# A two-layer hybrid backbone: S5 output operators on VectorE, and the second layer's operators made in the first layer's output projection

## The chip, the cores and the metric

The kernel runs on one core of one Trainium2 chip. The metric is device time in microseconds of one launch; each number of a run is the time of that one core. TensorE is called PE, VectorE DVE, ScalarE ACT, GpSimd POOL, and SyncE, which here only issues transfers, SP.

## The reference

Two layers over 256 context and 512 latent tokens of width 1024. Each layer normalises and modulates, projects into three groups of heads (SSD, GLA, S5), runs a scan in both directions in each, and projects the concatenation back with a gate and a residual. The change concerns the S5 group: 32 groups of 16 channels, each with 64 complex states per direction.

```python
lam_bar = jnp.exp(lam * jnp.exp(log_step[d])[:, None])
b_bar = ((lam_bar - 1.0) / lam)[..., None] * bmat
...
bu = jnp.einsum("blgh,gph->blgp", u.astype(jnp.complex64), b_bar)
h = s5_scan(bu, h0, lam_bar)      # h_t = lam_bar * h_{t-1} + bu_t
return jnp.einsum("blgp,ghp->blgh", h, cmat).real, h[:, -1]
...
for l in range(DEPTH):
    u_lat = rmsnorm(h_lat, norm_w[l]) * (1.0 + scale[:, None]) + shift[:, None]
    ...
    out_lat = jnp.concatenate([ssd_l, gla_l, s5_l], axis=-1) @ w_out[l]
    h_lat = h_lat + gate[:, None] * out_lat
return rmsnorm(h_lat, final_norm_w)
```

## The kernel before, in words

Everything is kept transposed, channels on the 128 partitions and tokens along the free axis. A product in 32 bits is three matmuls, since each operand is split into a high and a low part: `wsplit` (L409 to L417) loads a weight tile `wr` of 512 KB (L412), ACT copies it into `wh` (the copies of all helpers are recorded on L121), and a subtraction makes `wl` (L416), two times in three on POOL and once on DVE. The input projection's matmuls are L492 (latent tokens, tile `pl`) and L494 (context, `pc`), those of the output projection L1062 and L1064.

The S5 scan is done in blocks of eight tokens, 96 blocks in all. For that, operators are made from the parameters:

- `s5_lambda` (L253 to L349): some hundred small DVE operations that make the table of powers of `lam_bar`, `s5p` (128x576), and `l8` for the scan; PE transposes the powers, and they go to memory (`lpD`, L340).
- `s5_in_map` (L351 to L363), eight per layer: two loads of 512 KB (B, with each row sent to many partitions, and the powers), then six DVE operations of 128x512 (L360, L361 and L363, each twice). The result is the operator from eight tokens to a state; the matmuls L608 apply it, and DVE (L612, L613) and ACT put the result into the scan's tile `xy`.
- `s5_out_map` (L365 to L404), sixteen per layer: a load of C and B (L370), POOL's negation of a piece (L375) and six POOL operations of 128x288 that multiply the table with C (L380 to L385), a store of the result (`clD`, L388), 16 small PE matmuls (L394) into two tiles of the pool `pa` for the kernel inside a block of eight tokens, two ACT copies, two small DVE operations (L400, L401) and two stores (`gD`, L403 and L404). All of a map lies in one tile of the pool `cs`, which has three buffers.
- the scan itself is `carry` (L643 to L646) on DVE; the output matmuls L687 to L689 reload `clD` and `gD`.

Where things stand in the program: layer 0's eight input maps come ahead of its input projection, in the tiles `bA` and `bB`, with two tiles of the pool `bc` for their loads. Inside layer 0's input projection (L571 to L580) layer 1's lambda and eight input maps are made, in `bA`, and spilled to memory (`pwD`, `blD`); layer 1 loads them again (L602, L617). Layer 0's sixteen output maps come behind the loads of u (L594 to L596). Layer 1's sixteen output maps come behind layer 0's S5 output (L694 to L696), with the table loaded again (L669).

The output projection (`out_part`, L1053) has two halves. The first, over GLA and S5 channels, leaves partial sums in memory (`hpD`); then 16 rows of layer 1's modulation are made (L1089 to L1095); the second half is a loop over eight output blocks m (L1098 to L1114), each with a weight load, its matmuls, the partial sum's load and the residual on DVE (L1075, L1076). Then come the rest of the modulation, the norm of layer 1 (`norm_in`, L441) and layer 1 itself.

The order on each engine is not written by hand: a scheduler places the instructions when the kernel is built, by their order in the program and by when it takes their operands and buffers to be free. Once built, each engine goes through its instructions in that order. All loads and stores stand in SP's one queue, in order too.

Of the kernel before, what the change touches and what calls it, by code (L numbers as in the profile page):

```python
# [41 lines left out]
def hybrid_backbone_kernel(  # L42
# [17 lines left out]
    dma = nc.sync.dma_start  # L60
# [128 lines left out]
    pwD = dram([128, 704], "pwD1")  # L189
    blD = dram([8, 128, 1024], "blD1")  # L190
# [46 lines left out]
    pw0, l8_0 = T("s5p", [128, 576], 1), T("l8", [128, 128], 1)  # L237
# [126 lines left out]

    def s5_out_map(l, bi, pw, buf):  # L365

        gs = 2 * bi
        w5, tmp, cb, cn = cuts(buf, 576, 288, 128, 32)
# [9 lines left out]
        cr, ci, cm = (x.rearrange("p (g h) -> p g h", g=2).unsqueeze(2).to_broadcast(shp)  # L378
                      for x in (cb[:, 0:32], cb[:, 32:64], cn))
# [96 lines left out]
    def layer(l, u):  # L476
# [94 lines left out]
        wa = wa0 if not last else big("bA")  # L571
        if not last:
            sv, wk, lt, tw, tu, pwl = cuts(wa, 480, 512, 512, 576, 576, 704)
# [20 lines left out]
        if not last:  # L594
            for bi in range(16):
                s5_out_map(0, bi, pw_(pw0), cs())  # L596
        st = T("xy", [128, 8, NT], 1).rearrange("p a t -> p (a t)").rearrange("p (i r g) -> p i r g", i=96, r=2)
        for bi in range(16):
            if bi % 2 == 0:
                blt = bls[bi // 2] if not last else wa[:, 4096 + 1024 * (bi // 2 % 2) : 5120 + 1024 * (bi // 2 % 2)]  # L600
                if last:
                    dma(blt, blD[bi // 2])  # L602
            bl = blt.rearrange("p (a g x) -> p a g x", a=2, g=4)[:, :, 2 * (bi % 2) : 2 * (bi % 2) + 2, :]
# [10 lines left out]
        l8t = l8_0  # L614
        if last:
            l8t = T("l8", [128, 128], 1)
            dma(l8t, pwD[:, 576:704])  # L617
# [642 lines left out]
```

## Time and profile before

| | us |
|---|---|
| median of 3 runs (lowest, highest) | 1706.68 (1698.17, 1707.37) |
| the profiled execution | 1712.97 |
| its span | 1711.3 |
| PE busy | 1418.1 (83%) |
| DVE busy | 1168.2 (68%) |
| POOL busy | 783.2 (46%) |
| ACT busy | 679.9 (40%) |

The mean clock that PE was granted is 0.901 of its full speed. Busy shares are averages over stages with different limits. The stages that matter here, by time in the span: layer 0's input projection with the making of S5 operators, from 45 us on; a stretch from 480 to 640 us in which layer 1's output maps are made beside projections; layer 0's output projection, whose first half ends at about 943 us and whose second half ends at 1022; the norm of layer 1; and layer 1's projections and S5 scan behind it.

### The profile page before, as it was taken

The page shows a single profiled execution, that of the slowest core. Times are in us where ns is not written, and L with a number is a line of the kernel's source. Part 1 is how long each engine was busy: PE and PEld are TensorE (multiplying, and loading weights), DVE is VectorE, ACT ScalarE, POOL GpSimd, SP SyncE. Part 2 cuts the span into 40 slices and gives each one's busy share as a digit, 9 for nine tenths or more (in the row PEclk, how much of TensorE's full clock was granted, in tenths as well). Part 3 has the DMA queues.
Part 4 walks back from the last instruction along what each step waited for, and adds up shares of the span by engine and source line. Part 5 has one row for each costly group of instructions (what it writes and reads, how often), then busy time and mean ns, then how long its engine had stood idle before and what let it go on. Part 6 is the DMA issues. An engine that isn't in the chain of part 4 may idle for free.

```text
span 1711.3 us, 23539 instructions
## 1 busy us (share of the span) xinstructions
PE 1418.1 (83%) x8536; PEld 1145.2 (67%) x8536; DVE 1168.2 (68%) x1992; ACT 679.9 (40%) x1220; POOL 783.2 (46%) x716
## 2 busy tenths in 40 slices
PE   3867766888989779977779999997889989967886
PEld 2656655777966557755668786886678777745665
DVE  7977558995477567679994127289835986688752
ACT  4312223225342336646553124343345345545442
POOL 3615647632268843445463141164123323656454
PEclk9788987898988889988889999998988999988998
DMA  8474654332543354444455745522363242344542
GB/s 308 124 185 135 178 150 135 93 118 71 176 123 86 100 165 140 142 154 139 128 187 188 282 135 178 189 85 80 111 193 107 64 139 93 119 138 145 184 131 96
DMA packets 139885, 243.55 MB, mean 142 GB/s; under 512 B 31992, under 2 KB 72568, under 8 KB 139768
## 3 DMA queue, kind: packets, MB, share of 16 engines
q1 hardware_dynamic: 139768, 242.04, 45.3%
q8 instruction: 67, 1.10, 0.3%
q14 instruction: 50, 0.41, 0.1%
HBM read 192.81 MB, written 49.18 MB: 141 GB/s over the span
## 4 chain that ended last, share of the span: by engine, by line
PE 25%; DVE 18%; DMA 13%; POOL 6%; issue 4%; ACT 4%; SPq 0%; DVEq 0%; ACTq 0%; POOLq 0%
PE pl L492 7%; PE pl L1062 6%; DMA bA<-acsD 5%; DMA bB<-acsD 3%; PE pc L494 2%; PE pc L1064 2%; DVE xy L863 1%; DMA wr<-in_wblk 1%; ACT bA L121 1%; POOL wl L416 1%; DVE bB L916 1%; DVE bA L916 1%; DVE xy L645 1%; DMA cs<-zD 1%; DVE bA L644 1%
## 5 line engine op out<-in xcount | busy, mean ns | idle before, releaser
L492 PE MATMUL pl<-hl,wh 128*128 128x512 f32 (+1 forms) x1184 | 411.5, 414 | 15.9 <-DVE ev L511 12.3
L416 POOL TENSOR_TENSOR wl<-wr,wh 128x1024 fp32r<-128x1024 f32 (+1 forms) x82 | 210.4, 2566 | 308.5 <-ACT wh L121 284.6
L492 PEld LDWEIGHTS pl<-hl,wh 128*128 128x128 f32 (+1 forms) x1184 | 226.0, 195 | 73.5 <-DVE ev L511 13.6
L492 PE MATMUL pl<-hl,wl 128*128 128x512 f32 (+1 forms) x592 | 243.5, 412 | 20.0 <-POOL wl L416 10.7
L121 ACT ACTIVATE wh<-wr 128x1024 fp32r<-128x1024 f32 (+1 forms) x122 | 127.6, 1047 | 283.7 <-PE pc L1064 69.3
L494 PE MATMUL pc<-hl,wh 128*128 128x256 f32 (+1 forms) x864 | 202.0, 304 | 11.3 <-DVE ev L511 7.2
L494 PEld LDWEIGHTS pc<-hl,wh 128*128 128x128 f32 (+1 forms) x864 | 152.5, 202 | 26.1 <-DVE ev L511 8.7
L492 PEld LDWEIGHTS pl<-hl,wl 128*128 128x128 f32 (+1 forms) x592 | 115.4, 195 | 49.1 <-POOL wl L416 12.0
L494 PE MATMUL pc<-hl,wl 128*128 128x256 f32 (+1 forms) x432 | 128.6, 298 | 0.0
L1062 PE MATMUL pl<-hl,wh 128*128 128x512 f32 x256 | 87.7, 419 | 16.9 <-ACT hl L121 4.6
L394 PE MATMUL pa<-cs 64*32 64x128 f32 x512 | 42.9, 305 | 64.0 <-POOL cs L382 27.3
L494 PEld LDWEIGHTS pc<-hl,wl 128*128 128x128 f32 (+1 forms) x432 | 87.3, 202 | 2.7 <-issue 1.7
L121 ACT ACTIVATE ev<-pl 128x512 f32<-128x512 f32 (+1 forms) x96 | 51.1, 534 | 87.7 <-PE pl L709 43.9
L709 PE MATMUL pl<-wh,hl 128*128 128x256 f32 x384 | 79.6, 307 | 2.6 <-ACT ev L121 2.6
L416 DVE TENSOR_TENSOR wl<-wr,wh 128x1024 fp32r<-128x1024 f32 x40 | 55.4, 1386 | 38.3 <-ACT wh L121 38.1
L121 ACT ACTIVATE bB<-bB 128x512 f32<-128x512 f32 (+4 forms) x40 | 45.7, 1142 | 85.1 <-DMA bB<-acsD 52.3
L394 PEld LDWEIGHTS pa<-cs 64*32 64x32 f32 x512 | 21.5, 115 | 80.6 <-POOL cs L382 28.9
L863 DVE SCALAR_TENSOR_TENSOR xy<-ev,par_sb,xy 128x512 f32<-128x512 f32 (+1 forms) x112 | 74.8, 704 | 0.6
L375 POOL TENSOR_SCALAR cs<-cs 128x32 f32<-128x32 f32 x32 | 20.1, 629 | 118.4 <-DMA cs<-in_s5cb 43.3
L709 PEld LDWEIGHTS pl<-wh,hl 128*128 128x128 f32 x384 | 66.9, 214 | 7.8 <-ACT ev L121 3.8
L1062 PEld LDWEIGHTS pl<-hl,wh 128*128 128x128 f32 x256 | 49.8, 199 | 31.1 <-ACT hl L121 6.7
L709 PE MATMUL pl<-wl,hl 128*128 128x256 f32 x192 | 58.4, 308 | 3.8 <-DVE wl L416 3.8
(483 smaller groups left out, 3604.4 us busy)
## 6 DMA issues: line engine op xcount, KB each, us to landing
wr<-in_wblk SPq DMA_DIRECT2D x80, 512.0 KB
wr<-in_wout SPq DMA_DIRECT2D x32, 512.0 KB
hl<-in_mod_w SPq DMA_DIRECT2D x20, 512.0 KB
bA<-acsD SPq DMA_DIRECT2D x10, 1024.0 KB
bB<-acsD SPq DMA_DIRECT2D x10, 1024.0 KB
clD<-cs SPq DMA_DIRECT2D x64, 128.0 KB
cs<-clD SPq DMA_DIRECT2D x32, 256.0 KB
cs<-in_mod_w SPq DMA_DIRECT2D x16, 512.0 KB
```

Source lines behind the costliest of these rows:

```text
L121: return S.activation(out, in_, f, **kw)
L375: G.tensor_scalar(cn, cb[:, 0:32], -1.0, None, MUL)
L394: PE.matmul(pk[d][32 * gg : 32 * gg + 32], b0[64 * d : 64 * d + 64, a, :], w54[64 * d : 64 * d + 64, a, gg, d : 8 + d, :].rearrange("p k h ...
L416: (eng or (V if wcount[0] % 3 == 0 else G)).tensor_tensor(wl, wr, wh.bitcast(F32), SUB)
L492: PE.matmul(p_l[:m], lhs, u[k][:, ui, LC:NT], start=st, stop=sp)
L494: PE.matmul(p_c[:m], lhs, u[k][:, ui, 0:LC], start=st, stop=sp)
L644: V.tensor_tensor(tr[:, 1, :n], li, src[:, :, ::-1], MUL)
L709: PE.matmul(p, u[k][:, ui, 128 * c : 128 * c + 128], ws[k // 4][wi][:, 256 * (k % 4) : 256 * (k % 4) + 256], start=n == 0, stop=n == 23)
L863: V.scalar_tensor_tensor(ac, raw[:, o + k : o + k + n], pcol("cw", w0 + k), ac, MUL, ADD)
L916: V.scalar_tensor_tensor(rf[:, h, :], rbw[:, h, :], rb[:, ih : ih + 1], rf[:, h, :], SUB, MIN)
L1062: PE.matmul(p_l, lhs, rhs[kk][:, ui, LC - t0 : NT - t0], start=st, stop=sp)
L1064: PE.matmul(p_c, lhs, rhs[kk][:, ui, 0:LC], start=st, stop=sp)
```

## The change

It has four parts. (1) The six operations of `s5_out_map` go from POOL to DVE; the negation falls away, because the last operation, a `scalar_tensor_tensor`, now multiplies by −1. (2) Layer 1's lambda moves behind layer 1's first modulation rows, ahead of the second half of layer 0's output projection; its tables stay in SBUF (`s5p`, `l8`), with the tile `m12` for scratch. (3) Layer 1's eight input maps are made at the head of layer 1, behind its norm, by the same function as layer 0's (`s5_in_maps`), into `bA` and `bB`. They take both tiles of the pool `bc`, so that the loads of u, which use these tiles, come after. The spilled copies `pwD` and `blD` are gone. (4) Layer 1's sixteen output maps are made two by two in the loop over m of the second half of layer 0's output projection.

```diff
-    pwD = dram([128, 704], "pwD1")
-    blD = dram([8, 128, 1024], "blD1")
...
-    pw0, l8_0 = T("s5p", [128, 576], 1), T("l8", [128, 128], 1)
+    s5p = [(T("s5p", [128, 576], 1), T("l8", [128, 128], 1))]
...
+    def s5_in_maps(l):
+        t = [bct(), bct()]
+        wa, wb = big("bA"), big("bB")
+        out = [wb[:, 1024 * i : 1024 * i + 1024] for i in range(6)] + [wa[:, 1024 * i : 1024 * i + 1024] for i in range(2)]
+        for bi in range(8):
+            s5_in_map(l, bi, t[bi % 2][:, 0:1024], t[bi % 2][:, 1024:1536], wa[:, 2048:2560], out[bi])
+        return out
...
-        G.tensor_scalar(cn, cb[:, 0:32], -1.0, None, MUL)
...
-        G.tensor_tensor(w54[:, 0], pr, cr, MUL)
-        G.tensor_tensor(t54, pi, ci, MUL)
-        G.tensor_tensor(w54[:, 0], w54[:, 0], t54, SUB)
-        G.tensor_tensor(w54[:, 1], pi, cm, MUL)
-        G.tensor_tensor(t54, pr, ci, MUL)
-        G.tensor_tensor(w54[:, 1], w54[:, 1], t54, SUB)
+        V.tensor_tensor(w54[:, 0], pr, cr, MUL)
+        V.tensor_tensor(t54, pi, ci, MUL)
+        V.tensor_tensor(w54[:, 0], w54[:, 0], t54, SUB)
+        V.tensor_tensor(w54[:, 1], pi, cr, MUL)
+        V.tensor_tensor(t54, pr, ci, MUL)
+        V.scalar_tensor_tensor(w5[:, 288:576], w5[:, 288:576], -1.0, tmp, MUL, SUB)
...
-            s5_lambda(1, sv, wk, lt, tw, tu, pwl[:, 0:576], pwl[:, 576:704])
-            dma(pwD, pwl)
-            for bi in range(8):
-                lp = wa[:, 1024 * (bi % 2) : 1024 * (bi % 2) + 1024]
-                bb, tb, bl = cuts(wa[:, 2048:4096], 512, 512, 1024)
-                s5_in_map(1, bi, lp, bb, tb, bl)
-                dma(blD[bi], bl)
...
-            if bi % 2 == 0:
-                blt = bls[bi // 2] if not last else wa[:, 4096 + 1024 * (bi // 2 % 2) : 5120 + 1024 * (bi // 2 % 2)]
-                if last:
-                    dma(blt, blD[bi // 2])
...
-        if not last:
-            pw1 = T("s5p", [128, 576], 1)
-            dma(pw1, pwD[:, 0:576])
...
-        if not last:
-            for bi in range(16):
-                s5_out_map(1, bi, pw_(pw1), cs())
...
             mod_scale(1)
+
+            s5p.append((T("s5p", [128, 576], 1), T("l8", [128, 128], 1)))
+            s5_lambda(1, *cuts(m12(), 480, 512, 512, 576, 576), *s5p[1])
         hx2 = T("xy", [128, 8, NT], 1)
         acc = None
         for m in range(8):
...
+            if not last:
+                for bi in (2 * m, 2 * m + 1):
+                    s5_out_map(1, bi, pw_(s5p[1][0]), cs())
...
     u = norm_in(1, hx, nrm)
+    bls = s5_in_maps(1)
     hx, acc = layer(1, u)
```

In the changed kernel the lines of these functions stand five further down (L380 becomes L385, L412 becomes L417), those of the S5 scan 12 or more further up (L620 becomes L608), those of the output projection 15 further up (L1104 becomes L1089).

**The order on DVE and POOL while layer 0's output maps are made.** On POOL before, in layer 0's input projection (`cs` is a map's tile, `s5p` the table, `wl` a weight split):

```order
L416 TENSOR_TENSOR wl_2659<-wr_2656,wh_2658 128x1024
L375 TENSOR_SCALAR cs_1399<-cs_1399 128x32
L380 TENSOR_TENSOR cs_1399<-s5p_139,cs_1399 128x288
L381 TENSOR_TENSOR cs_1399<-s5p_139,cs_1399 128x288
L383 TENSOR_TENSOR cs_1399<-s5p_139,cs_1399 128x288
L382 TENSOR_TENSOR cs_1399<-cs_1399 128x288
L375 TENSOR_SCALAR cs_1426<-cs_1426 128x32
L380 TENSOR_TENSOR cs_1426<-s5p_139,cs_1426 128x288
```

On DVE with the change, at the first three maps of layer 0, beside its input maps (`bA`, `bB`, `bc`):

```order
L358 TENSOR_TENSOR bB_483<-bc_481 128x512 x2
L385 TENSOR_TENSOR cs_911<-s5p_137,cs_911 128x288
L386 TENSOR_TENSOR cs_911<-s5p_137,cs_911 128x288
L388 TENSOR_TENSOR cs_911<-s5p_137,cs_911 128x288
L385 TENSOR_TENSOR cs_937<-s5p_137,cs_937 128x288
...
L361 TENSOR_TENSOR bB_483<-bB_483,bA_482 128x512
L387 TENSOR_TENSOR cs_911<-cs_911 128x288
...
L421 TENSOR_TENSOR wl_731<-wr_728,wh_730 128x1024
L359 TENSOR_TENSOR bA_482<-bc_480 128x512
L389 TENSOR_TENSOR cs_911<-s5p_137,cs_911 128x288
```

POOL's maps stood between its weight splits; now they stand on DVE between input maps, weight splits and the projection's own operations, and three maps are begun together.

**The order on SP in the second half of layer 0's output projection.** Before (`wr` are the projection's weights, `cv` the partial sums, `h1D` the stored result, `hl` weights of the modulation):

```order
L412 DMA wr_7784<-in_wout 128x1024
L1092 DMA hl_7522<-in_mod_w 128x1024
L1104 DMA h1D<-xy_7535 128x512
L412 DMA wr_7846<-in_wout 128x1024
L1104 DMA h1D<-xy_7535 128x512
L412 DMA wr_7908<-in_wout 128x1024
```

With the change:

```order
L417 DMA wr_7698<-in_wout 128x1024
L1086 DMA cv_7639<-hpD_127 128x768
L408 DMA gD_135<-cs_7076 16x240
L409 DMA gD_135<-cs_7076 16x240
L376 DMA cs_7216<-in_s5cb 128x128
L408 DMA gD_135<-cs_7102 16x240
L409 DMA gD_135<-cs_7102 16x240
L1089 DMA h1D<-xy_7013 128x512
L376 DMA cs_7304<-in_s5cb 128x128
L393 DMA clD_133<-cs_7216 256x1x128 x2
L417 DMA wr_7813<-in_wout 128x1024
```

Between two weight loads there now stand loads of maps and stores of their results. About 7 of the 16 maps' PE rows stand behind the last row of the projection.

**The order on DVE at the head of layer 1.** Before, the last operations of the norm (L473) are followed at once by the first copy of the S5 scan (L620, of `l8`):

```order
L473 SCALAR_TENSOR_TENSOR hl_8132<-bA_8088,modp,hl_8132 128x512
L473 SCALAR_TENSOR_TENSOR hl_8137<-cv_8099,modp,hl_8137 128x256
L473 SCALAR_TENSOR_TENSOR hl_8137<-cv_8099,modp,hl_8137 128x512
L620 COPY cs_8659<-l_854_8657 128x128
L530 COPY m_804_8211<-pa_8215 128x192
```

With the change (the end of the eight input maps, then the copies of L608's results into `xy`):

```order
L421 TENSOR_TENSOR wl_8991<-wr_8988,wh_8990 128x1024
L361 TENSOR_TENSOR bA_8051<-bA_8051 128x512
L358 TENSOR_TENSOR bA_8051<-bc_8050 128x512
L359 TENSOR_TENSOR bA_8051<-bc_8050 128x512
L358 TENSOR_TENSOR bA_8051<-bc_8050 128x512
L361 TENSOR_TENSOR bA_8051<-bA_8051 128x512
L359 TENSOR_TENSOR bA_8051<-bc_8050 128x512
L361 TENSOR_TENSOR bA_8051<-bA_8051 128x512
L608 COPY cs_8609<-l_685_6895 128x128
L603 COPY xy_8480<-ps_8489 64x64x2
```

All 48 operations of the eight input maps stand on DVE ahead of the first copy of a result.

## Rows read from the trace of the kernel before

**Rows 1.** The page: busy time, share of the span and instructions by engine.

```profile
PE 1418.1 (83%) x8536; PEld 1145.2 (67%) x8536; DVE 1168.2 (68%) x1992; ACT 679.9 (40%) x1220; POOL 783.2 (46%) x716
```

**Rows 2.** Span and mean granted clock of the core.

```profile
core 0: 1711.3 us, clock 0.901
```

**Rows 3.** Windows by stage: stretch, length, busy time by engine (instructions).

```profile
core 0: us, PE busy (x) PEld busy (x) DVE busy (x) ACT busy (x) POOL busy (x), PEclk, DMA share, GB/s
45.00:300.00 255.00, 188.73 (x1184) 153.02 (x1185) 181.31 (x332) 64.51 (x128) 134.52 (x131) 0.84 0.56 152
...
480.00:640.00 160.00, 125.56 (x847) 96.64 (x846) 109.44 (x190) 51.37 (x107) 114.69 (x141) 0.86 0.41 114
...
900.00:1020.00 120.00, 119.30 (x747) 97.36 (x746) 31.27 (x43) 28.53 (x32) 38.15 (x18) 1.00 0.57 206
...
1050.00:1130.00 80.00, 79.73 (x511) 70.28 (x509) 33.46 (x65) 26.75 (x49) 23.70 (x19) 1.00 0.53 171
1130.00:1230.00 100.00, 81.39 (x466) 68.03 (x466) 98.31 (x138) 34.33 (x47) 40.78 (x29) 0.90 0.29 92
```

**Rows 4.** Waits of PE, 45 to 300 us: total us, times, longest.

```profile
PE pa L394 <- POOL cs L382: 27.0, 6, 9.4
...
PE pa L394 <- DVE cs L400: 12.9, 6, 5.3
...
PE pa L394 <- POOL cs L385: 3.3, 2, 2.8
```

**Rows 5.** Waits of PE, 480 to 640 us.

```profile
PE pa L394 <- ACT cs L121: 18.7, 3, 11.8
PE pl L492 <- POOL wl L416: 9.7, 2, 9.0
...
PE pa L394 <- DVE cs L400: 1.7, 2, 0.9
```

**Rows 6.** Chain that ended last, 480 to 640 us: start, us.

```profile
515.79 1.73 DMA cs<-in_s5cb
...
574.82 3.35 POOL cs L375
```

**Rows 7.** Window 45 to 300 us, POOL's work on tile cs alone.

```profile
45.00:300.00 255.00, 102.92 (x112) 0.84 0.56 152
```

**Rows 8.** Timeline of DVE in layer 1's scan: start, us.

```profile
1157.49 0.21 DVE L644 TENSOR_TENSOR bA<-cs,xy 128x64 f32<-128x64 f32 x1
1157.62 0.21 DVE L645 TENSOR_TENSOR xy<-xy,bA 128x64 f32<-128x64 f32 x1
...
1221.05 0.68 DVE L646 TENSOR_TENSOR xy<-xy,bA 128x512 f32<-128x512 f32 x1
1221.65 0.68 DVE L643 TENSOR_TENSOR bA<-cs,xy 128x512 f32<-128x512 f32 x1
```

**Rows 9.** Window 45 to 160 us, DVE's work on tile bA alone.

```profile
45.00:160.00 115.00, 57.60 (x142) 0.84 0.57 149
```

**Rows 10.** DVE on tile bA: ns min/median/max, first and last start.

```profile
L361 DVE TENSOR_TENSOR bA<-bc x16: 674/681/1186, 59.6 to 129.6; 128x512 f32<-128x512 f32 x16
```

**Rows 11.** Groups of DVE by form, 45 to 300 us.

```profile
L361 DVE TENSOR_TENSOR bA<-bA 128x512 f32<-128x512 f32 x16 | 18.2, 1135 | 25.8 <-DMA bA<-in_s5b 15.5 <-issue 10.2
```

**Rows 12.** Window 45 to 300 us, POOL's weight splits L416 alone.

```profile
45.00:300.00 255.00, 24.96 (x10) 0.84 0.56 152
```

**Rows 13.** Window 480 to 640 us, PE's matmuls L394 alone.

```profile
480.00:640.00 160.00, 19.24 (x252) 0.86 0.41 114
```

**Rows 14.** Waits of SP's queue, 480 to 640 us: total us, times, longest.

```profile
SPq L403 <- DVE cs L401: 36.3, 12, 7.3
```

**Rows 15.** Residual of the second half of layer 0's output projection.

```profile
L1076 DVE SCALAR_TENSOR_TENSOR xy<-pl,modp,cv x8: 750/751/752, 956.5 to 1022.3; 128x512 f32<-128x512 f32 x8
```

**Rows 16.** PE on L608, the first S5 input matmuls of layer 1.

```profile
L608 PE MATMUL pa<-bc,bA x64: 243/275/275, 1084.9 to 1116.7; 128*128 128x96 f32 x64
```

More of the change, by code (lines that the diff above doesn't have):

```diff
@@ L363, in s5_in_map @@
             V.tensor_tensor(blo, blo, tb, SUB if o == 0 else ADD)
+    def s5_in_maps(l):
[5 more added lines that the diff above has]
+        return out
     def s5_out_map(l, bi, pw, buf):
         gs = 2 * bi
-        w5, tmp, cb, cn = cuts(buf, 576, 288, 128, 32)
+        w5, tmp, cb = cuts(buf, 576, 288, 128)
         gt = tmp[:, 0:240]
@@ L374, in s5_out_map @@
         t54 = tmp.rearrange("p (g k h) -> p g k h", g=2, k=9)
-        G.tensor_scalar(cn, cb[:, 0:32], -1.0, None, MUL)
         shp = [128, 2, 9, 16]
         pr, pi = (pw[:, :, a, gs : gs + 2].rearrange("p k g -> p g k").unsqueeze(3).to_broadcast(shp) for a in range(2))
-        cr, ci, cm = (x.rearrange("p (g h) -> p g h", g=2).unsqueeze(2).to_broadcast(shp)
-                      for x in (cb[:, 0:32], cb[:, 32:64], cn))
-        G.tensor_tensor(w54[:, 0], pr, cr, MUL)
-        G.tensor_tensor(t54, pi, ci, MUL)
-        G.tensor_tensor(w54[:, 0], w54[:, 0], t54, SUB)
-        G.tensor_tensor(w54[:, 1], pi, cm, MUL)
-        G.tensor_tensor(t54, pr, ci, MUL)
-        G.tensor_tensor(w54[:, 1], w54[:, 1], t54, SUB)
+        cr, ci = (x.rearrange("p (g h) -> p g h", g=2).unsqueeze(2).to_broadcast(shp)
+                  for x in (cb[:, 0:32], cb[:, 32:64]))
+        V.tensor_tensor(w54[:, 0], pr, cr, MUL)
[4 more added lines that the diff above has]
+        V.scalar_tensor_tensor(w5[:, 288:576], w5[:, 288:576], -1.0, tmp, MUL, SUB)
         for d in range(2):
@@ L568, in layer @@
             dma(acsD[l][:, d].rearrange("c h l -> h c l"), rows.rearrange("h (c l) -> h c l", c=6))
-        wa = wa0 if not last else big("bA")
-        if not last:
-            sv, wk, lt, tw, tu, pwl = cuts(wa, 480, 512, 512, 576, 576, 704)
-            s5_lambda(1, sv, wk, lt, tw, tu, pwl[:, 0:576], pwl[:, 576:704])
-            dma(pwD, pwl)
-            for bi in range(8):
-                lp = wa[:, 1024 * (bi % 2) : 1024 * (bi % 2) + 1024]
-                bb, tb, bl = cuts(wa[:, 2048:4096], 512, 512, 1024)
-                s5_in_map(1, bi, lp, bb, tb, bl)
-                dma(blD[bi], bl)
         for i in range(4):
@@ L595, in layer @@
             for bi in range(16):
[L596 removed]
+                s5_out_map(0, bi, pw_(s5p[0][0]), cs())
         st = T("xy", [128, 8, NT], 1).rearrange("p a t -> p (a t)").rearrange("p (i r g) -> p i r g", i=96, r=2)
         for bi in range(16):
[L599 to L603 removed]
+            bl = bls[bi // 2].rearrange("p (a g x) -> p a g x", a=2, g=4)[:, :, 2 * (bi % 2) : 2 * (bi % 2) + 2, :]
             pst = (px, ps)[bi % 2](384)
@@ L613, in layer @@
             V.tensor_copy(st[64:128, 32:96, :, gsl], pv[64:128, 95:31:-1])
[L614 to L617, printed above, removed]
+        l8t = s5p[l][1]
         pt8 = cs().rearrange("p (k a r) -> p k a r", k=8, a=2)
@@ L692, in layer @@
                 dma(y5D[l][b4 // 2].rearrange("t (h g) c -> (t h) g c", h=16), y5[:, 4 * b4 - 4 : 4 * b4 + 4, :])
-        if not last:
-            for bi in range(16):
-                s5_out_map(1, bi, pw_(pw1), cs())
         for i in range(4):
@@ L1112, in layer @@
             if m == 6:
-                act(ho[:, 0:1] if last else T("l8", [128, 128], 1)[:, 0:1], acc[:, 0:1], AF.Ln, scale=0.0, bias=1.0)
+                act(ho[:, 0:1], acc[:, 0:1], AF.Ln, scale=0.0, bias=1.0)
+            if not last:
+                for bi in (2 * m, 2 * m + 1):
+                    s5_out_map(1, bi, pw_(s5p[1][0]), cs())
         return hx2, (acc, sq)
@@ L1130, in hybrid_backbone_kernel @@
     rsqrt_rows(buf[0])
-    s5_lambda(0, cs(), cs(), cs(512), cs(), cs(), pw0, l8_0)
+    s5_lambda(0, cs(), cs(), cs(512), cs(), cs(), *s5p[0])
     tA, tB = big("bA"), big("bB")
@@ L1149, in hybrid_backbone_kernel @@
     u = norm_in(0, hx, nrm)
-    t = [bct(), bct()]
-    wa0, wb0 = big("bA"), big("bB")
-    bls = [wb0[:, 1024 * i : 1024 * i + 1024] for i in range(6)] + [wa0[:, 4096 + 1024 * i : 5120 + 1024 * i] for i in range(2)]
-    lps, bbs = [a[:, 0:1024] for a in t], [a[:, 1024:1536] for a in t]
-    for bi in range(8):
-        s5_in_map(0, bi, lps[bi % 2], bbs[bi % 2], wa0[:, 3360:3872], bls[bi])
+    bls = s5_in_maps(0)
     hx, acc = layer(0, u)
```

## The prediction

> **What bounds the kernel now.** I read the table of engines first. The reader is to see that TensorE (PE) is busy 83% of the span, VectorE (DVE) 68% and GpSimd (POOL) 46% [rows 1]: the program is bounded by PE work and by the holes in it, and the engine that takes the moved work is the fuller one. The mean clock granted to PE is 0.901 [rows 2]. Next comes the table by stretches [rows 3]. In layer 0's input projection (45 to 300 us) PE is busy 188.73 of 255 us at clock 0.84; after layer 0's S5 output (480 to 640) 125.56 of 160 at 0.86. In both stretches output operators are made. In the second half of layer 0's output projection (900 to 1020), where the change puts layer 1's, PE is busy 119.30 of 120 us at clock 1.00, with DVE at only 31.27. The head of layer 1 (1050 to 1130) has no hole in PE either, but 46.5 us free on DVE. From 1130 to 1230 DVE is busy 98.31 of 100 and PE 81.39: the S5 scan.
>
> Then I read what PE waits for. In the first stretch the waits of the maps' own matmuls L394 (for L382, L400 and L385) come to 27.0 + 12.9 + 3.3 = 43.2 us [rows 4], of 66.3 that PE is idle; in the second, L394 waits 18.7 and 1.7 and the projection waits 9.7 for a POOL weight split, 30.1 together [rows 5] of 34.4 idle. The chain that ended last passes through the load of an output map and through POOL's negation L375, which took 3.35 us with its wait [rows 6]. So PE, which takes its instructions in order, stands in front of a map that POOL has not yet made. POOL spends 102.92 us on the 16 maps of the first stretch [rows 7], 6.4 us each.
>
> **The change part by part.** The sum is made against the profiled execution, 1712.97 us, which lies 6.3 above the median of the runs, 1706.68.
>
> *(a) Layer 0's maps on DVE.* Six 128x288 operations per map. No DVE row has this shape: back to back, a 128x512 takes 1221.65 − 1221.05 = 0.60 us and a 128x64 takes 0.13 [rows 8]; the line between gives 0.365, so 6 × 0.365 = 2.2 us per map and 35 per layer. DVE's load in this stretch does not grow: layer 1's lambda leaves it (at most 47 us: the 57.6 of DVE's work on tile bA up to 160 us [rows 9], less 16 operations of layer 0's input maps at 0.681 [rows 10]) and so do 48 input-map operations, at 0.60 us or more 29, against 35 that come. POOL loses 102.92. A map takes a third of its former time, so a third of the 43.2 us of waiting stays: **−29** [0 to −43]. For scale, the input maps' subtraction on DVE averages 1135 ns there [rows 11], against 0.68 us for a single one of the same shape in the scan [rows 8]: something slows DVE while POOL is at work.
>
> The Trainium skill (SBUF — State Buffer, § Who interferes with whom) has a rule that speaks against the change: a VectorE instruction with two SBUF inputs contends with a GpSimd instruction that reads SBUF. The 1135 ns fit it, without proving it. By it the moved operations would sometimes sit out one of POOL's ten remaining splits in the stretch, which take 24.96 us [rows 12]; were all of that lost, the term would be about −4 and the sum −21 instead of −46.
>
> *(b) Layer 1's maps leave the second stretch.* Their waits go, all three: −18.7 − 1.7 − 9.7 = **−30** [−20 if a projection split is late instead, −30].
>
> *(c) Their PE work moves.* It takes 19.24 us there [rows 13], at clock 0.86, and comes back where PE has no hole, at 1.00: 19.24 × 0.86 = 16.5. **−19 + 17**. Some 7 of the 16 maps land behind the output projection, among the norm and the first projections, which are full as well.
>
> *(d) Clock.* With fewer holes the two stretches may rise to the mean clock: 188.73 × (1 − 0.84/0.90) = 12.6 and 106 × (1 − 0.86/0.90) = 4.7, 17 together (106 is what is left of 125.56 after (c)). I take **−10** [0 to −17], since part of the holes stays.
>
> *(e) DMA issue in the output projection.* The new stores gD and clD and the loads of the maps stand in SP's queue, in order, between the weight loads of the projection. In the second stretch SP waited 36.3 us for line L401's results, 12 times, 3.0 on average, 7.3 at most [rows 14]. Behind such a store the next weight tile waits. A block of the projection lasts (1022.3 − 956.5)/7 = 9.4 us [rows 15] and holds two maps, so 6 us of waiting on average, and there are two weight buffers, so most of it is hidden: **+10** [0 to +36]. DVE itself has room: 35 us of maps and at most 47 of lambda are 82, against 88.7 idle in 900 to 1020. The lambda is therefore costed at nothing; without that cover it would cost up to its 47, since every map needs its table.
>
> *(f) Input maps at the head of layer 1.* Now 48 DVE operations stand between the norm and the S5 input matmuls L608. Best: 48 × 0.60 = 29 us, which fits into the 46.5 idle ones: 0. Worst: the pace of layer 0's maps, 59.6 to 129.6 us for eight [rows 10], 70 us, begun at 1050: L608 then starts at 1120 instead of 1084.9 [rows 16], 35 later, and the scan that DVE bounds with it; the 7 late output maps add 7 × 2.2 = 15. Loads of u for these matmuls wait for the same two buffers. DVE's free time nearly covers the best case plus the late maps (44 of 46.5), so I stay nearer that end: **+15** [0 to +50]. What leaves with the spilled tables (the loads of 512 KB input maps, and their stores) is hidden and costed at nothing: the DMA share there is 0.53.
>
> Sum: −29 − 30 − 19 + 17 − 10 + 10 + 15 = **−46**: 1667 on the profiled execution's scale, **1661** on that of the median.
>
> **The rivals.**
> *The holes close fully.* (a) −43, (b) −30, (c) −2, (d) −17, (e) and (f) 0: −92, about 1615. For it: DVE is a third of POOL's time per operation. Against: PE also waits 12.9 us for DVE's own L400, and those chains through PSUM and ACT stay. It is the low end of the forecast's case, not a case apart.
>
> *No change: DVE takes POOL's place.* In the first stretch DVE was busy 181.31 of 255, and the maps are queued on it among norm, projection and input-map work; if PE then waits on DVE as long as it did on POOL, (a) and (d) are 0: −30 − 19 + 17 + 10 + 15 = −7, about 1700. For it: DVE is the fuller engine, and its order already shows three maps begun together and finished only behind a 128x512 operation and a weight split. Against: its load there falls. The Trainium skill (Perfetto Trace Analysis, § Optimizing Scalar/DVE Operations) gives that rule: the two share an SBUF read port, "so offloading operations between those two might not help". Chance 0.13.
>
> *Slower: SP's in-order queue starves the output projection.* Each map's stores hold the weight load behind them. Fourteen of the sixteen maps would have to do so for about 6 us: 84 instead of the 10 of (e) gives +28, about 1735. It decides for slower from some 4 us per map (56 instead of 10 makes the sum 0). For it: PE has no hole there to give (119.30 of 120), so any late weight is paid in full. Against: the mean wait was 3.0 us, and 7.3 the longest. Chance 0.11.
>
> *The change does not do what it says.* The order shows all maps and the lambda where the change puts them, but for the 7 late ones, which (c) and (f) hold; no chance of its own.
>
> **How the numbers follow.** About 0.5% (8.5 us) is what a measurement of this kernel can tell from no change. The forecast with its own range is faster, 0.76; no change 0.13; slower 0.11. The low end is −92 with the runs' scatter, 1612. Upward, (e) and (f) at half of their bounds (18 and 25), (a) at a third of its size (−10) and (d) at half (−5) make the sum −10 − 30 − 2 − 5 + 18 + 25 = −4, so 1703 takes in the no-change case and leaves the slower one out.
>
> **What would show it.** Right: PE's idle time in the first stretch falls from 66 us to about 35 and L394's waits on POOL are gone; the second stretch is some 50 us shorter; the output projection grows by about 17 to 27 us and stays full; L608 of layer 1 begins at most 15 us later than its stretch did. Wrong: waits of L394 on DVE that add up to 40 us in the first stretch (the second rival), projection matmuls L1062 waiting for weights or splits in the output projection (the third), or holes in PE before layer 1's L608.

## The result, and the profile after

The changed kernel takes 1720.97 us (median of 5 runs, 1715.71 to 1723.95), the kernel before 1705.95 (5 runs). The ratio is 1.0102, with a 95% interval of 1.0065 to 1.0138: slower by 1%. The forecast was 1661 us, faster, with a range of 1612 to 1703.

The page of the changed kernel, its time by engine; then its span and clock; then the windows that answer to [rows 3]:

```profile
PE 1415.7 (82%) x8536; PEld 1141.4 (66%) x8536; DVE 1209.7 (70%) x2184; ACT 681.8 (40%) x1220; POOL 596.5 (35%) x492
```

```profile
core 0: 1716.9 us, clock 0.906
```

```profile
45.00:300.00 255.00, 216.94 (x1393) 175.16 (x1391) 197.28 (x375) 75.76 (x145) 71.03 (x50) 0.91 0.46 126
...
480.00:640.00 160.00, 146.60 (x828) 124.83 (x826) 126.60 (x223) 84.77 (x176) 51.62 (x54) 0.95 0.32 107
```

POOL gave up 187 us and DVE took 42. In both stretches in which the sum looked for its gain, PE is fuller: 216.94 us instead of 188.73, and 146.60 instead of 125.56. PE's waits for the maps in the first stretch, 43.2 us in [rows 4], have become these:

```profile
PE pa L399 <- DVE cs L405: 5.5, 3, 3.2
...
PE pa L399 <- DVE cs L390: 1.5, 2, 1.1
```

So what was looked at went as forecast, and the time did not. The two traces have to be laid side by side at the same places of the program, not at the same microseconds: the end of layer 0's output projection, and the end of layer 1's S5 scan. Three windows of the kernel before:

```profile
0.00:1022.40 1022.40, 825.12 (x5286) 666.43 (x5289) 701.14 (x1262) 378.00 (x704) 507.45 (x490) 0.89 0.49 152
1022.40:1225.90 203.50, 181.20 (x1098) 149.21 (x1098) 150.74 (x231) 73.42 (x116) 66.52 (x50) 0.93 0.41 131
1225.90:1711.30 485.40, 411.74 (x2158) 329.52 (x2157) 316.38 (x501) 228.52 (x401) 209.25 (x176) 0.91 0.41 127
```

The same three of the changed kernel:

```profile
0.00:982.60 982.60, 807.34 (x5187) 656.71 (x5188) 698.25 (x1363) 379.60 (x694) 322.04 (x266) 0.91 0.46 144
982.60:1256.70 274.10, 224.47 (x1335) 178.25 (x1334) 205.93 (x339) 82.56 (x138) 75.59 (x64) 0.91 0.43 125
1256.70:1716.90 460.20, 383.86 (x2018) 306.40 (x2016) 305.56 (x483) 219.63 (x390) 198.85 (x162) 0.91 0.41 127
```

Layer 0 ends 40 us earlier, the stretch to the end of layer 1's scan is 71 us longer, and the last one 25 us shorter. PE's work in all is the same (1418 and 1416 us), so length less PE's busy time is the honest column: PE idles 197, 22 and 74 us before, 175, 50 and 76 after. Layer 0 won 22 us of holes instead of the 60 or so that the sum counted, and the head of layer 1 lost 27.

At single places of the changed kernel (the residual of the projection's second half, and the last S5 input matmuls of layer 1):

```profile
L1058 DVE SCALAR_TENSOR_TENSOR xy<-pl,modp,cv x8: 734/746/751, 896.7 to 986.5; 128x512 f32<-128x512 f32 x8
```

```profile
L599 PE MATMUL pa<-bc,bA x16: 248/275/275, 1139.5 to 1141.1; 128*128 128x96 f32 x16
```

The seven blocks between the first and the last residual take 89.8 us instead of 65.8 [rows 15]. The S5 input matmuls end 24 us later than in [rows 16], although the projection ahead of them ended 40 us earlier.

### The profile page after: what moved, and what is told of

Read it like the earlier page. It is cut to its first block, busy times and chain, and to the rows that moved or that the text cites. A ratio compares the mean times of both kernels' runs of the same rounds, so it can differ in the third digit from the quotient of the medians.

```text
span 1716.9 us, 23372 instructions
## 1 busy us (share of the span) xinstructions
PE 1415.7 (82%) x8536; PEld 1141.4 (66%) x8536; DVE 1209.7 (70%) x2184; ACT 681.8 (40%) x1220; POOL 596.5 (35%) x492
## 4 chain that ended last, share of the span: by engine, by line
DVE 32%; PE 28%; DMA 19%; issue 7%; ACT 6%; POOL 4%; SPq 1%; DVEq 0%; ACTq 0%; POOLq 0%
PE pl L497 7%; PE pl L1044 5%; DMA bB<-acsD 5%; DMA bc<-lpD 4%; PE pc L499 3%; DMA bA<-acsD 3%; DMA cs<-in_mod_w 3%; DVE xy L845 2%; PE pc L1046 2%; ACT bA L121 2%; DVE xy L633 2%; DVE xy L634 2%; PE pl L691 1%; DMA cs<-in_s5cb 1%; DVE bB L898 1%
## 5 line engine op out<-in xcount | busy, mean ns | idle before, releaser
L499 PE MATMUL pc<-hl,wh 128*128 128x256 f32 (+1 forms) x864 | 211.5, 315 | 4.4 <-DVE ev L516 3.2
L499 PEld LDWEIGHTS pc<-hl,wh 128*128 128x128 f32 (+1 forms) x864 | 160.8, 212 | 20.5 <-issue 9.3
L499 PE MATMUL pc<-hl,wl 128*128 128x256 f32 (+1 forms) x432 | 133.6, 310 | 0.0
L1044 PE MATMUL pl<-hl,wh 128*128 128x512 f32 x256 | 88.3, 421 | 15.8 <-ACT hl L121 4.6
L499 PEld LDWEIGHTS pc<-hl,wl 128*128 128x128 f32 (+1 forms) x432 | 90.9, 210 | 4.6 <-issue 3.2
L845 DVE SCALAR_TENSOR_TENSOR xy<-ev,par_sb,xy 128x512 f32<-128x512 f32 (+1 forms) x112 | 81.6, 756 | 0.8
L691 PE MATMUL pl<-wh,hl 128*128 128x256 f32 x384 | 73.5, 291 | 0.0
L691 PEld LDWEIGHTS pl<-wh,hl 128*128 128x128 f32 x384 | 61.1, 195 | 4.7 <-ACT bB L121 3.0
L1008 PE MATMUL pl<-hl,wh 128*128 128x512 f32 x128 | 48.2, 443 | 11.3 <-ACT cv L121 8.0
L1044 PE MATMUL pl<-hl,wl 128*128 128x512 f32 x128 | 53.2, 415 | 3.2 <-DVE wl L421 2.0
L121 ACT ACTIVATE bA<-bA 128x512 f32<-128x512 f32 (+2 forms) x30 | 23.5, 784 | 79.6 <-DMA bA<-acsD 59.1
```

The lines of the kernel that those rows point to most:

```text
L121: return S.activation(out, in_, f, **kw)
L499: PE.matmul(p_c[:m], lhs, u[k][:, ui, 0:LC], start=st, stop=sp)
L691: PE.matmul(p, u[k][:, ui, 128 * c : 128 * c + 128], ws[k // 4][wi][:, 256 * (k % 4) : 256 * (k % 4) + 256], start=n == 0, stop=n == 23)
L845: V.scalar_tensor_tensor(ac, raw[:, o + k : o + k + n], pcol("cw", w0 + k), ac, MUL, ADD)
L1008: PE.matmul(p_l, lhs, yg5[k][:, ui, LC:NT], start=n == 0, stop=n == 11)
L1044: PE.matmul(p_l, lhs, rhs[kk][:, ui, LC - t0 : NT - t0], start=st, stop=sp)
```

## The experiments

Four parts can be put in or left out: **D**, the maps' operations on DVE; **M**, layer 1's output maps moved to the output projection; **I**, its input maps at the head of layer 1; **L**, its lambda in the output projection. Where L is left out, the lambda stays in layer 0's input projection and its tables are spilled and loaded again. Ratios are to the kernel before as measured beside the run; its median lay between 1703 and 1707 us, so small differences are read from the ratios and not from the times.

**D alone.** The kernel before, with

```diff
-        G.tensor_tensor(w54[:, 0], pr, cr, MUL)
+        V.tensor_tensor(w54[:, 0], pr, cr, MUL)
...
-        G.tensor_tensor(w54[:, 1], w54[:, 1], t54, SUB)
+        V.scalar_tensor_tensor(w5[:, 288:576], w5[:, 288:576], -1.0, tmp, MUL, SUB)
```

> The kernel before with one part of the change alone: the six operations of the output maps on VectorE, everything else in its old place. Theory A (the moved work is not what cost; the eight input maps at the head of layer 1, paced by their loads, gave the gain back): the waits of PE on POOL for the maps go in both stretches, VectorE keeps the 40 us of lambda and the input maps in the first stretch, so 1665 to 1690 us. Theory B (VectorE is the fuller engine, and what POOL gives up it pays for in the SSD stage that it bounds): 1700 us or more.

Measured: 1711.24 us, ratio 1.0016 [0.9993, 1.0039]: no change. PE's waits in its first stretch, 45 to 300 us:

```profile
PE pc L493 <- DVE ev L510: 8.9, 1, 8.9
PE pl L491 <- DVE wl L415: 8.6, 2, 4.6
...
PE pa L393 <- DVE cs L381: 3.7, 2, 2.7
PE pa L393 <- issue: 3.2, 3, 1.6
PE pa L393 <- DVE cs L384: 2.3, 4, 1.4
```

Its windows, and the second of them in the kernel before:

```profile
45.00:300.00 255.00, 204.01 (x1269) 163.46 (x1270) 193.80 (x432) 68.06 (x133) 47.29 (x32) 0.88 0.60 162
300.00:480.00 180.00, 147.44 (x956) 129.18 (x955) 131.67 (x233) 63.81 (x74) 57.18 (x67) 0.85 0.32 98
```

```profile
300.00:480.00 180.00, 159.88 (x1054) 139.79 (x1053) 127.36 (x223) 66.37 (x81) 74.58 (x92) 0.91 0.38 118
```

Of the 43.2 us of waits for the maps about 10 are left. PE is 15 us busier in the first window and 12 us less busy in the next one. The last step of layer 0's scan begins at 403 us, before at 402: the scan runs on DVE, and DVE, in its own order, stands in front of the spills and loads of layer 1's input maps:

```profile
DVE bA L360 <- DMA blD<-bA: 16.0, 6, 6.5
DVE bA L361 <- DMA bA<-in_s5b: 14.7, 5, 4.5
DVE bB L360 <- DMA bc<-lpD: 13.8, 3, 5.0
```

PE did its projections sooner, and the scan, with all that follows from it, came no earlier. This is argued from the two times of the scan: no row shows PE waiting for it, and PE's longest wait in the second window is one of 10.9 us for a weight split. Where the input maps have left layer 0 (runs below), the last step of the scan begins at 352 us with the maps on POOL (I), at 339 on DVE (D and I) and at 336 with M as well. Theory A falls (no gain). B's number came true, but the time does not lie where B put it: the SSD stage is as long as before (210 us from its first matmul to that of the output projection, before 208).

**M alone, D and M.** The second is the first with D:

```diff
-            for bi in range(16):
-                s5_out_map(1, bi, pw_(pw1), cs())
...
+            pw1 = T("s5p", [128, 576], 1)
+            dma(pw1, pwD[:, 0:576])
         hx2 = T("xy", [128, 8, NT], 1)
...
+                for bi in (2 * m, 2 * m + 1):
+                    s5_out_map(1, bi, pw_(pw1), cs())
```

> The kernel before with the sixteen output maps of layer 1 in the loop of layer 0's output projection, still on POOL, their table loaded there; lambda and input maps in their old place, spilled. Theory A: the second stretch loses its 30 us of waits and 19 of PE work, the projection grows by about 20 us and, with POOL at 6.4 us per map, by up to 30 more: 1680 to 1710 us. Theory B: a pure gain, below 1680, since nothing is put on VectorE.

> The kernel before with both parts: output maps on VectorE and layer 1's in the output projection; lambda and input maps of layer 1 stay in layer 0's input projection and are spilled and reloaded as before. Theory A: the head of layer 1 is as short as before (the first S5 input matmuls end about 68 us behind the norm, not 123), so 1645 to 1675 us, some 50 us under the whole change. Theory B: no better than the whole change by more than 10 us, 1705 to 1720.

Measured: M 1751.7, ratio 1.0249 [1.0215, 1.0283]; D and M 1719.35, 1.0060 [1.0037, 1.0083]. Both expectations of theory A fail; theory B fails for M, and for D and M its range holds. On POOL the maps are too slow for a projection of 80 us: it ends at 1002 us, 21 earlier than before, but the last map's matmul stands at 1079, and all behind the projection takes 745 us instead of 689. With D the projection ends 22 us earlier than with D alone (1007 against 1029 us), and all behind it is 28 us longer (711 against 683). Maps that land behind the projection (the last matmul at 1058) stand in the queues of layer 1; whether they cost the 28 us is asked below. One store of `gD` held SP for 16.2 us there:

```profile
SPq L402 <- DVE cs L400: 20.4, 5, 16.2
```

**D, M and I** (the change without L).

```diff
-            s5_lambda(1, *cuts(m12(), 480, 512, 512, 576, 576), *s5p[1])
+            for t_, z_ in zip(s5p[1], (slice(0, 576), slice(576, 704))):
+                dma(t_, pwD[:, z_])
...
+            s5_lambda(1, sv, wk, lt, tw, tu, pwl[:, 0:576], pwl[:, 576:704])
+            dma(pwD, pwl)
         for i in range(4):
             p_c, p_l = proj(BU + i, early=last and i == 0)
```

> The changed kernel with layer 1's lambda made in layer 0's input projection and its tables spilled and reloaded in the output projection; the input maps stay at the head of layer 1. Theory A: the head still gives the gain back, 1700 to 1715 us. Theory C (the lambda's 40 us of VectorE, which run in the SSD stage that VectorE bounds, are what the change lost): 1675 to 1690.

Measured: 1692.55, ratio 0.9906 [0.9877, 0.9936]: 1% faster than the kernel before, and 28 us faster than the whole change. It lies 2.6 us above theory C's range and 7 below A's: A falls, and the gain is nearly of the size that C gives. Its three windows, cut at the same places:

```profile
0.00:961.60 961.60, 798.57 (x5187) 648.77 (x5188) 683.67 (x1357) 375.95 (x692) 327.06 (x266) 0.92 0.48 148
961.60:1228.60 267.00, 228.39 (x1358) 181.42 (x1356) 206.57 (x346) 84.14 (x140) 76.78 (x65) 0.90 0.43 129
1228.60:1687.90 459.30, 383.26 (x1995) 303.78 (x1994) 307.17 (x483) 217.82 (x387) 200.58 (x162) 0.91 0.41 127
```

PE idles 163, 39 and 76 us. Of the 29 us between the profiled runs 21 lie ahead of the projection's end. In the changed kernel DVE works on the lambda's scratch (tile m) from 767 to 850 us, not in the free DVE time of 900 to 1020:

```profile
600.00:880.00 280.00, 37.02 (x103) 0.90 0.46 149
```

This is the SSD norm and the first half of the projection, where DVE is nearly full (80.1 of the 83 us from 767 to 850 are busy). Layer 0's scan gains from the lambda's leaving, by 10 us (its last step begins at 327 us, 336 without L), and what follows loses more than that. Many of these small operations sit out a POOL operation. DVE, then POOL, in the same stretch (start, us):

```profile
785.18 0.18 DVE L249 SCALAR_TENSOR_TENSOR m<-m 128x32 f32<-128x32 f32 x1
785.28 0.95 DVE L950 TENSOR_TENSOR xy<-xy,cs 128x768 f32<-128x768 f32 x1
786.15 2.27 DVE L249 SCALAR_TENSOR_TENSOR m<-m 128x32 f32<-128x32 f32 x1
```

```profile
785.96 2.42 POOL L426 TENSOR_TENSOR hl<-cv,hl 128x768 fp32r<-128x768 f32 x1 [4.37 <-ACT hl L121]
```

The same operation takes 0.18 us and, begun while POOL works, 2.27, and ends with POOL's at 788.4.

**A second lambda**, whose results nothing uses, on D, M and I:

```diff
+            sv, wk, tw, tu, pj, lj = cuts(m12(), 480, 512, 576, 576, 576, 128)
+            s5_lambda(1, sv, wk, tu[:, 0:512], tw, tu, pj, lj, ld=2)
             s5p.append((T("s5p", [128, 576], 1), T("l8", [128, 128], 1)))
```

> The run with the early lambda (1692.55 us) plus a second lambda of layer 1, made where the change makes it, whose results nothing uses. Theory C1 (the lambda's work on VectorE, among the SSD and norm operations of layer 0, is what costs the 28 us): 1710 to 1722, as the whole change. Theory C2 (the wait for the table is what costs: the output maps, which need it, come late): 1690 to 1700.

Measured: 1714.7 (1698.27 to 1731.25), ratio 1.0042 [1.0013, 1.0072]; the median lies where C1 put it. The projection with it and without it:

```profile
778.80:979.50 200.70, 176.58 (x1068) 136.81 (x1069) 111.62 (x234) 50.55 (x73) 53.35 (x24) 0.91 0.51 166
```

```profile
780.80:961.50 180.70, 165.65 (x1064) 130.31 (x1065) 87.16 (x142) 49.08 (x71) 61.07 (x24) 0.98 0.55 181
```

DVE has 24 us more to do, and the stretch is 20 us longer, 9 of them PE's holes and 11 its lower clock. The work alone thus costs 1.4% of the 2.0% between 0.9906 and 1.0102. The rest I can't assign: part of it lies ahead of the lambda, where the new order differs as well.

**I alone, D and I.** Output maps in their old places; the first with POOL, the second with DVE:

```diff
+    bls = s5_in_maps(1)
     hx, acc = layer(1, u)
```

> The kernel before with one part alone: layer 1's eight input maps at the head of layer 1 (lambda stays in layer 0's input projection and is spilled; output maps on POOL, in their old places). Theory D (the parts add up: VectorE for the output maps 0 to +5 us, output maps in the output projection +5, input maps at the head of layer 1 -30, lambda in the output projection +29, by the four runs so far): 1670 to 1685. Theory E (the input maps' move gains only because the waits of the output maps on POOL are gone too): 1695 to 1715.

> The same with the output maps on VectorE. Theory D: 1670 to 1690, within 6 us of the run on POOL. Theory E: at least 15 us faster than the run on POOL, since with the input maps gone VectorE has the room and PE's waits are on the path.

Measured: I 1727.84, ratio 1.0127 [1.0091, 1.0164]; D and I 1723.5, 1.0100 [1.0070, 1.0130]. Theories D and E both fall: the parts do not add up. The input maps' move loses 0.8% (beside D) to 1.3% (alone) when the output maps stay, and wins 1.5% when they have moved (1.0060 to 0.9906). PE's holes in the traces, all beside D, show where: in layer 0, up to the projection's end, I takes 27 us of them (200 to 173), M 12 (to 187.5), both 37 (to 163). From there to the end of layer 1's scan I adds 26 (17 to 43), M 17 (to 34), and both only 22 (to 39): ahead they add up, behind they share one hole. In time, beside D: the projection's end comes 29 us earlier with I, 22 with M and 68 with both, and what lies behind it becomes 40, 28 and 43 us longer.

**The whole change with the maps on POOL.**

> The whole change with the output maps back on POOL. If the six operations on VectorE are worth something only together with the other parts (PE's waits for the maps are on the path once layer 0's scan is no longer late and the maps stand in the full projection): 1740 to 1760, as the move alone on POOL was 32 us slower than on VectorE. If they are worth nothing here either: 1715 to 1725.

Measured: 1751.2, ratio 1.0270 [1.0216, 1.0323], as the first case said. So D is worth 1.7% inside the change and 1.9% beside M alone (1.0249 to 1.0060); where the output maps stay in their old places it is worth nothing that can be told from zero, alone (1.0016) or beside I (1.0127 to 1.0100, with intervals that overlap). The gain does not lie in layer 0: with the maps on POOL the projection's last matmul even stands at 975 us, with D at 982. It lies behind that point, where the last map's matmul stands at 1080 us with POOL and at 1035 with D. PE's waits for the maps in the 100 us behind the projection, with POOL, then with D:

```profile
PE pa L400 <- POOL cs L388: 15.4, 2, 12.0
PE pa L400 <- POOL cs L391: 8.0, 3, 4.3
```

```profile
PE pa L399 <- DVE cs L387: 4.0, 1, 4.0
PE pa L399 <- DVE cs L390: 1.8, 1, 1.8
```

Of the two conditions in the first case it is thus the place of the maps that counts: beside I alone layer 0's scan is no longer late either, and D gains nothing.

**The output maps in the first half of the projection**, on D, M and I:

```diff
         def spilled_part(src, k0, rhs, order):
...
                 dma(hpD[l][128 * m : 128 * m + 128, t0:NT], ho[:, t0:NT])
+                if not last:
+                    for bi in (2 * m, 2 * m + 1):
+                        s5_out_map(1, bi, pw_(s5p[1][0]), cs())
```

> The run with the early lambda (1692.55 us), with layer 1's output maps in the loop of the first half of layer 0's output projection instead of the second, so that none is left for the head of layer 1. Theory F (the maps that land behind the projection hold up SP's queue and VectorE at the head of layer 1, and cost the 28 us that this stretch lost when the maps moved): 1655 to 1675. Theory G (the maps' PE work and transfers cost where there is no hole, wherever that is, or the first half, which VectorE bounds, pays as much): 1685 to 1705.

Measured: 1698.08, ratio 0.9946 [0.9916, 0.9976]; theory G, and no gain over D, M and I (0.9906). No map is left for layer 1, its S5 scan ends 40 us earlier (1189 instead of 1229 us), and what follows is 53 us longer:

```profile
972.00:1188.70 216.70, 181.02 (x1075) 147.31 (x1073) 182.19 (x273) 74.28 (x116) 68.43 (x50) 0.91 0.38 117
1188.70:1701.40 512.70, 425.79 (x2180) 338.43 (x2180) 321.59 (x506) 224.00 (x397) 204.66 (x177) 0.89 0.40 124
```

The end of layer 1's scan does not set the end of the program: PE has 2180 matmuls left at that point, and 1995 in the run with the maps in the second half.

**What the input maps cost at the head.** Five runs. Without six of the eight loads of B, on the whole change; without both loads of six maps, on D, M and I:

```diff
+        if l == 0 or bi < 2:
             dma(bb, bass.AP(tensor=s5b.tensor, ...
```

> The whole change without six of the eight loads of B for layer 1's input maps (the maps 2 to 7 of layer 1 use the B of maps 0 and 1). Theory H (the maps at the head follow each other at 10 us because of their two loads of 512 KB each): the maps are 6 to 8 us apart, the S5 input matmuls end 15 to 25 us earlier, and the time is 8 to 20 us under the whole change: 1700 to 1713. Theory I (the queue and the late output maps set the pace): within 5 us of the whole change.

> The run with the early lambda (1692.55 us) without the loads of layer 1's input maps 2 to 7 (both of them: these maps are made of the operands of maps 0 and 1). If the maps' loads make the hole at the head of layer 1: PE idles there 15 us less and the time is 1670 to 1682. If the hole is made of other waits in the in-order queues (late output maps, modulation loads, VectorE's scan): 1686 to 1697.

Measured, without the loads of B: 1713.99, ratio 1.0054 [1.0033, 1.0075], 7 us under the whole change, between the two theories, with intervals that overlap. H's sign is not there: the S5 input matmuls end at 1141 us as in the whole change. Without both loads: 1699.51, 0.9971 [0.9958, 0.9983]: above both ranges and not faster than with the loads, 7 us slower, although the S5 input matmuls end 10 us earlier (with the loads, then without):

```profile
L608 PE MATMUL pa<-bc,bA x16: 248/275/275, 1111.4 to 1113.0; 128*128 128x96 f32 x16
```

```profile
L610 PE MATMUL pa<-bc,bA x16: 246/275/275, 1101.4 to 1103.4; 128*128 128x96 f32 x16
```

The loads hold up the maps (in the changed kernel DVE waits 21.7 + 8.1 us for them, below), but making the maps faster by their loads wins nothing.

```profile
DVE bB L358 <- DMA bc<-lpD: 21.7, 4, 6.6
DVE bA L358 <- DMA bc<-lpD: 8.1, 2, 4.4
```

Four buffers for the loads (`t += [t2[:, 0:1536], t2[:, 1536:3072]]` with `t2 = m12()`), the last modulation rows ahead of the loop (`mod_tiles(1, 16, 8)` behind `mod_scale(1)`), and both, each on D, M and I:

> The run with the early lambda, with four buffers instead of two for the loads of layer 1's input maps (two more in the scratch tile m12). If the maps' loads set the length of the hole at the head of layer 1: the S5 input matmuls end 20 us or more earlier and the time is 1675 to 1687. If PE's order and VectorE's scan set it: within 5 us of 1692.

> The run with the early lambda, with the last rows of layer 1's modulation (eight loads of 512 KB into the pool of the output maps, and their PE rows) ahead of the loop instead of behind it. If PE's 8.5 us of waits for these loads at the head are on the path: 1680 to 1688. If they only stand in for another wait: 1689 to 1697.

> Four buffers for the input maps' loads and the last modulation rows ahead of the loop, both on the run with the early lambda. Four buffers alone cost 30 us, with 22 us of PE waits for the modulation's loads at the head. If that was the cause (the maps' loads, issued earlier, stand in front of the modulation's in SP's queue): 1680 to 1695, as those loads are then gone from the head. If the four buffers cost by something else (the scratch tile that they take, or the order that they lead to): 1710 or more.

Measured: four buffers 1722.51, ratio 1.0109 [1.0067, 1.0152], outside both cases, with the S5 input matmuls no earlier (1115 us); modulation ahead 1691.27, 0.9926 [0.9901, 0.9952]; both 1721.98, 1.0087 [1.0072, 1.0102]. The modulation's loads were not on the path, nor are they what the four buffers held up. Why these cost 30 us (their tile m12 is also the SSD part's scratch) was not found out.

The tile bB: held in the kernel before, by one word, and freed in the run with the maps in the first half:

```diff
-        wa = wa0 if not last else big("bA")
+        wa = wa0 if not last else big("bB")
```

```diff
+        out = [big6[:, 1024 * i : 1024 * i + 1024] for i in range(6)]
+        out += [cs(), cs()] if l else [wa[:, 1024 * i : 1024 * i + 1024] for i in range(2)]
```

> The kernel before with one word changed: layer 1's reloaded input maps lie in the tile bB instead of bA, so that bB is taken until the last S5 input matmul of layer 1. Theory J (what the input maps at the head of layer 1 cost is not their loads nor their work, but the tile bB: the GLA part, which begins in that tile, starts behind the last of these matmuls, some 60 to 80 us later than before, and PE has less to do during the S5 scan): 1725 to 1745 us. Theory K (the tile does not matter; the maps' operations on VectorE and the later scan do): 1700 to 1712.

> The run with the early lambda and the output maps in the first half of the projection (1698 us), with layer 1's input maps made into bA and two tiles of the pool cs, their scratch in PSUM, so that bB is free for the GLA part. Theory J: the GLA part starts 40 us or more earlier in layer 1 and the time is 1660 to 1682. Theory K: 1690 to 1705.

Measured: bB held 1704.5, ratio 0.9996 [0.9975, 1.0018]; bB freed 1691.12, 0.9909 [0.9871, 0.9946], its interval overlapping that of the run it was made from (0.9946). Both lie in theory K's ranges, and J falls: with bB held, the GLA part's load of `lrD` into it is issued at 1108.6 us instead of 1054.9, and the time is the same.

Six of the eight input maps left out, on the same run:

```diff
+        if l:
+            out = [out[6], out[7]] * 4
+        for bi in range(2 if l else 8):
```

> The run with the early lambda and the output maps in the first half of the projection (1698 us), with only two of layer 1's eight input maps made; its S5 input matmuls use these two, four times over. Left out are 36 operations of VectorE, the loads of six maps, and the wait for them. Theory K (the maps' own work and the later S5 scan cost the 40 us at the head): 1655 to 1675. If it stays at 1690 or more, the maps at the head are not what costs, and the length of layer 1 is set by something that no run here has touched.

Measured: 1680.99, ratio 0.9839 [0.9814, 0.9865], 17 us under the run with all eight, between the two cases. The S5 input matmuls end 24 us earlier (1054 instead of 1078). The loads alone were worth nothing on D, M and I, so what is left are DVE's 36 operations and the wait behind them; they were not taken out by themselves.

## Why the prediction was wrong

Its sum has terms for what lies ahead of the end of layer 0's output projection, (a) to (e), and one for what lies behind it, (f). The run without L tells them from the lambda, which the sum costed at nothing.

**Ahead of the projection's end: the total right, two steps wrong in it.** (a) to (e) give −29 − 30 − 19 + 17 − 10 + 10 = −61; the projection's last matmul moved from 1022.1 to 961.4 us, by −61, in the run without L. That is a coincidence. The step "a third of the 43.2 us of waiting stays: −29" fails: D alone took these waits down to about 10 us, and the projection's end came no earlier (1029 us). A wait of PE was priced as time, although layer 0's scan, on which the next stage hangs, stayed as late as it was. Beside I, where the scan is early, D brings the projection's end forward by 13 us (1013 to 1000), and in the whole change not at all (975 without D, 982 with it). Its 1.7% there is earned behind the projection, by keeping the moved maps out of layer 1; the sum has no such term. And the step "What leaves with the spilled tables … is hidden and costed at nothing" fails: the leaving of the input maps brings the projection's end forward by 9 us alone, by 29 beside D, and from 1007 to 961 us beside D and M.

The other terms ahead of that end did better. (b), (c) and (e): M moved it by 22 us beside D, and −30 − 19 + 17 + 10 is −22, although a part of the moved PE work lies behind that end. The second half of the projection became 20 us longer (from 943.5 to 1022.4 us before, from 883.7 to 982.7 now), against 17 + 10: PE, which had no idle time there, is busy 94 of 99 us, so some 15 us are work and 5 are holes. (d): the clock in the windows of the two stretches rose (0.84 to 0.91, 0.86 to 0.95; they hold other work by now), but the mean only from 0.901 to 0.906, and PE's busy time fell by 2.4 us, not by 12, −10 of which was for the clock: mis-sized.

**"The lambda is therefore costed at nothing"** is the step that turned the sign. The cover named, DVE's idle time in 900 to 1020 us, is not where the lambda runs. Nothing in the program holds it back, so the scheduler put it as early as its scratch tile is free: the load of its parameters is issued at 759.1 us, right behind the last matmul that reads that tile for other work (758.8). That is a stretch where DVE has little room (in the kernel before, 94 of the 100 us from 800 to 900 are busy). Without that cover the prediction said "up to its 47"; the run without L is 28 us faster. The price of the moved map operations, on the other hand, was nearly right: a 128x288 takes 0.37 us back to back, where 0.365 was worked out; some took longer beside POOL (below), so that the 192 records average 0.51 us where an undisturbed one shows 0.45.

**(f) was mis-sized.** From the projection's end to the end of the program it was 689 us before and 726 without L, +37 instead of +15, inside the bound of 50. Of the reasons given, the pace of the loads is not one: without the loads nothing is won. DVE's operations ahead of L608 are a part of it: six maps left out win 17 us. But an earlier end of the scan was given back where the output maps moved to the first half. What makes the rest of the 37 stays open.

The stretches as measured: −61 + 21 (L ahead of the projection's end) + 8 (L behind it) + 37 (f) = +5, which by construction is what the profiled executions did (1712.97 to 1718.59, +5.6). Without the lambda's 29 the change is faster, as forecast, but by 14 us (medians) or 23 (profiled executions) instead of 46.

**The rivals.** The one on the slow side put the blame on SP's queue in the projection; the projection grew as the forecast had it, and none of PE's waits in its second half (5.1 us in all) is for a weight, so that was not the mechanism. A store that held SP for 16.2 us exists, at the head of layer 1. The one for no change (DVE takes POOL's place) is what D alone does, but for another reason than it gave: PE hardly waits for DVE's maps, and the scan comes no earlier. The rule weighed in (a), from the Trainium skill (SBUF — State Buffer, § Who interferes with whom), is borne out by the two timelines above for a DVE operation that reads two SBUF operands, 0.18 us against 2.27. Such waits make the small operations of the lambda dear, where the sum had no term for them, and lengthen some of the maps' operations too.

## What to carry to other kernels

A wait of the fullest engine is worth its time only if what ends the stretch comes earlier with it: look for the engine that the next stage hangs on, and lay two traces side by side by places of the program and by length less busy time. Before costing moved work at nothing, find in the new order the stretch in which it will really stand; a scheduler that puts it as early as it can puts it among what is full. Measure the parts of a change apart and in pairs: here one part was worth nothing alone and 1.7% with the others, and the version without the fourth part beats both kernels (1692.55 us, ratio 0.9906).

## What the runs showed of the hardware

A DVE operation of 128x32 takes 0.18 us, and 1.2 to 2.4 us where it begins during a POOL operation, up to that one's end. Operations with one operand from SBUF show it too: a `tensor_scalar` of the lambda took 1.24 and 2.38 us, the same kind elsewhere in it 0.17 (ns min/median/max):

```profile
L241 DVE TENSOR_SCALAR m<-m x2: 1237/1806/2375, 772.5 to 792.1; 128x32 f32<-128x32 f32 x2
...
L245 DVE TENSOR_SCALAR m<-m x2: 174/178/181, 782.9 to 802.0; 128x32 f32<-128x32 f32 x2
```

Some of the maps' 128x288 operations were held in the same way, 2.08 us instead of 0.45 (start, us; DVE, then POOL):

```profile
975.36 0.45 DVE L385 TENSOR_TENSOR cs<-s5p,cs 128x288 f32<-128x288 f32 x1
975.73 2.08 DVE L386 TENSOR_TENSOR cs<-s5p,cs 128x288 f32<-128x288 f32 x1
```

```profile
975.66 1.84 POOL L443 TENSOR_TENSOR ev<-ev,cv 128x768 f32<-128x768 f32 x1 [4.89 <-ACT cv L121]
```

The prediction had priced the maps' operations at their undisturbed length.
